# The up projection of the MLP as seven half-sized products with weight sums made in DRAM

## The chip, the cores and the metric

The kernel runs on one core of a Trainium2 chip. The metric is the device time of one execution in microseconds (us). All times are of this kernel with one set of inputs, and every array is float32.

## The reference

One decoder layer over 512 tokens of 1024 features. A combined input projection feeds three attention branches (differential, stick-breaking, dilated) and three gates; their merged output goes through a projection and a LayerNorm. Then comes the part that the change is about:

```python
x = layer_norm(DEEPNORM_ALPHA * x + m, ln1_g[i], ln1_b[i])
hid = jax.nn.relu(x @ w_up[i])                 # (512,1024) @ (1024,4096)
c = jnp.square(hid) @ w_down[i]                # (512,4096) @ (4096,1024)
ple = jax.nn.sigmoid(x @ w_ple_gate[i]) * (p[i] @ w_ple[i])
x = layer_norm(DEEPNORM_ALPHA * x + c + ple, ln2_g[i], ln2_b[i])
```

## The kernel before

**Products in three passes.** Each float32 factor is split into a high part in float32r and a low part (value minus high part, also in float32r). A product is hi x hi + hi x lo + lo x hi, three matmuls (`mm3`, L88 to L90) that accumulate in PSUM. A weight chunk of 128 x 1024 floats is loaded by SyncE into one of 7 `raw` buffers (`fill`, L162), cast to `wh` by ACT (L206) and subtracted to `wl` by DVE (L208). `wh` and `wl` have 7 buffers each; the split of a chunk may be written to the queues up to 7 chunks ahead of what the items have released (`pump`).

**Items.** The work of TensorE is a list of items, each with the chunks that it needs, a function `mm` that issues matmuls and a function `ev` that empties the bank. The loop at the end (L1352) goes through the list: it makes sure that the chunks are split, writes the previous item's `ev`, and then the item's `mm`. A scheduler then orders the instructions of each engine, so matmuls of neighbouring items can be interleaved. Items use two PSUM banks in turn (`mm_bank`); six more (`at_bank`) serve attention and long sums.

**MLP.** After the input projection, attention, the branches, the per-layer embedding (`ple_items`), the output projection (`wout_items`) and the gate (`pleg_items`) come `mlp_items`. The transposed input `x1T` (8 tiles of 128 features x 512 tokens, high and low part `x1Tl`) is made in `ln1_gen`. The up projection has 32 items `up(f)`, one for each 128 hidden columns: 8 feature tiles x 3 matmuls of 512 columns (tokens). Its `ev` makes relu and square on ACT.

The down projection is done in pairs of hidden tiles with a scheme of seven products for a 2 x 2 block product (in place of eight): tokens are cut in halves `HB` and `HC`, output columns in halves of 512. `left_first` and `left_rest` make the sums of the hidden activations on DVE and split them. `wsum` holds four sums of weight blocks for each of 7 groups of two pairs. They are made in DRAM by DMAs on POOL's queue: `sum_steps` copies a block and adds others to it in the transfer (L593, L595), 8 steps a group, one step per item from item 30 on, each tied to the latest `wl` subtraction. `down(b, p, r, c)` is product p for token tile r of its half: p = 1, 6, 7 stay in PSUM over all groups, the others are added to `acc` by DVE (L705) in each group. The eighth group is done in the plain way (`plain`), whose items also hold the second LayerNorm; the last item is cut in parts of 512, 256 and 256 columns.

**POOL's other work.** The loads of `pT` (L1000), of the LayerNorm constants (`ln_consts`) and of `xn`, and the power -0.5 of each LayerNorm (L440, L458) are on POOL's queue too, behind the sum steps that were written before them.

Of the kernel before, what the change touches and what calls it, by code (L numbers as in the profile page):

```python
# [56 lines left out]
def trunk(tc, a, out):  # L57
    nc = tc.nc
    es = ExitStack()
    with es:  # L60
# [7 lines left out]
        NSLOT = 42  # L68
# [74 lines left out]
        RING, RAW = 7, 7  # L143
# [332 lines left out]
        ln1_done = {}  # L476

# [22 lines left out]
        def ln1_gen(tt):  # L500
# [11 lines left out]
            for h in range(2):  # L512
# [7 lines left out]
            ln1_done[tt] = True  # L520
            yield
# [23 lines left out]
        def pleg_items():  # L545
            for half in range(2):
                cs = [chunk(a["wg"][half, c].rearrange("p k n -> p (k n)"), 1024) for c in range(4)]
                for tt in range(4):
# [9 lines left out]
                    def ev(ps, tt=tt, half=half):  # L558
# [6 lines left out]
                        if half and tt > 1:  # L565
                            nc.vector.tensor_sub(acc[tt - 2, 1], acc[tt - 2, 1], t)
# [9 lines left out]
        wsum = [[dram.tile([P, 1024], F32, name=f"wsum{b}_{i}") for i in range(4)] for b in range(7)]  # L576

        def sum_steps():
            def steps(b):
                w = [a["wd"][b, i].rearrange("p k n -> p (k n)") for i in range(4)]  # L580
                t = wsum[b]
                yield t[0], w[0], False
                yield t[2], w[1], False
                yield t[0], w[1], True
                yield t[2], w[3], True
                yield t[1], t[0], False
                yield t[1], w[3], True
                yield t[3], t[1], False
                yield t[3], w[2], True
# [10 lines left out]
            todo = deque(steps(b) for b in range(7))  # L600
            run = []
            while todo or run:
                while todo and len(run) < 3:
# [9 lines left out]
        hraw = {}  # L613
        later = deque()
        left = {}
        keep = {}
        p1s = {}
        v3 = {}
        HB = slice(0, 256)
        HC = slice(256, 512)  # L620

        def mlp_items():
            nb = 7

            def up(f, free=True):
                c = chunk(a["wu"][f].rearrange("p k m -> p (k m)"), 1024)

                def mm(ps):
                    for k in range(8):
                        s = slice(k * P, k * P + P)  # L630
                        mm3(ps, c["h"][:, s], c["l"][:, s], x1T[k], x1Tl[k], k == 0, k == 7)

                def ev(ps):
                    t = slot("hid")
                    nc.scalar.activation(t, ps, AF.Relu)
                    nc.scalar.activation(t, t, AF.Square)
                    left_rest()
                    if f >= 4 * nb:
                        left[f] = split(t)
                        return  # L640
                    hraw[f] = t
                    if f % 2:
                        left_first(f // 2)
                item([c] if free else [], mm, ev)
                return c

            def split(t, cols=slice(0, 512)):
                h = slot("hh", F32R)
                lo = slot("hl", F32R)
                nc.scalar.copy(h[:, cols], t[:, cols])  # L650
                nc.vector.tensor_sub(lo[:, cols], t[:, cols], h[:, cols].bitcast(F32))
                return h, lo

            def left_first(pr):
                e, o = hraw[2 * pr], hraw[2 * pr + 1]
                s12 = slot("s12")
                nc.vector.tensor_sub(s12[:, HB], e[:, HC], o[:, HC])
                nc.vector.tensor_sub(s12[:, HC], e[:, HB], s12[:, HB])
                w = slot("hh", F32R)
# [843 lines left out]
```

## Time and profile before

| what | value |
|---|---|
| median of 3 runs | 1081.71 us (1080.97 to 1082.08) |
| the profiled execution's time | 1082.02 us |
| its span, first to last instruction | 1080.1 us |
| granted TensorE clock | 0.998 |
| TensorE busy, share of the span | 99% |
| DVE, ACT, POOL busy | 61%, 44%, 6% |
| bytes read and written in HBM | 143.21 MB, 31.48 MB |

The span is shorter than the time by 1.9 us, which lie outside the first and last instruction. In a row of the timeline the first number is the start in us from the span's beginning, the second the duration; PE is TensorE's matmuls, PEld its weight loads. In a group's row the numbers behind the bar are the busy time in us and the mean duration of one in ns, then the idle time before it and what ended it. Matmuls are pipelined: the next starts before the last has ended, so their pace is read from their starts.

### The profile page before, as it was taken

The page shows a single profiled execution, that of the slowest core. Times are in us where ns is not written, and L with a number is a line of the kernel's source. Part 1 is how long each engine was busy: PE and PEld are TensorE (multiplying, and loading weights), DVE is VectorE, ACT ScalarE, POOL GpSimd, SP SyncE. Part 2 cuts the span into 40 slices and gives each one's busy share as a digit, 9 for nine tenths or more (in the row PEclk, how much of TensorE's full clock was granted, in tenths as well). Part 3 has the DMA queues.
Part 4 walks back from the last instruction along what each step waited for, and adds up shares of the span by engine and source line. Part 5 has one row for each costly group of instructions (what it writes and reads, how often), then busy time and mean ns, then how long its engine had stood idle before and what let it go on. Part 6 is the DMA issues. An engine that isn't in the chain of part 4 may idle for free.

```text
span 1080.1 us, 13246 instructions
## 1 busy us (share of the span) xinstructions
PE 1069.5 (99%) x4986; PEld 893.5 (83%) x4986; DVE 661.1 (61%) x1223; ACT 478.5 (44%) x795; POOL 70.0 (6%) x111
## 2 busy tenths in 40 slices
PE   9999999999999999999999999999999999999997
PEld 6888788999888888888888888888888888888886
DVE  6888667547254757655443464864575575575676
ACT  6665545425232545464233332233555454454441
POOL 0000200000111011111110020110000000000000
PEclk9999999999999999999999999999999999999999
DMA  8332313153675354567873262242244343444302
GB/s 311 129 117 90 118 40 98 51 183 98 144 208 154 119 127 166 141 162 198 244 193 111 102 231 81 89 166 98 98 158 135 137 156 136 138 146 142 122 1 78
DMA packets 43520, 146.18 MB, mean 135 GB/s; under 512 B 5593, under 2 KB 6505, under 8 KB 43457
## 3 DMA queue, kind: packets, MB, share of 16 engines
q1 hardware_dynamic: 32448, 107.93, 29.4%
q0 software_dynamic: 10432, 36.50, 13.5%
q8 instruction: 39, 0.64, 0.2%
q10 hardware_dynamic: 576, 0.92, 0.2%
q14 instruction: 25, 0.20, 0.1%
HBM read 143.21 MB, written 31.48 MB: 162 GB/s over the span
## 4 chain that ended last, share of the span: by engine, by line
PE 96%; DVE 2%; DMA 1%; ACT 0%; issue 0%; SPq 0%; DVEq 0%
PE mm L88 18%; PE mm L89 18%; PE mm L90 18%; PE mm L317 3%; PE mm L319 3%; PE mm L318 3%; PE mm L698 2%; PE mm L699 2%; PE mm L700 2%; PE at L698 2%; PE at L699 2%; PE at L700 2%; PE mm L556 1%; PE mm L490 1%; PE mm L488 1%; PE mm L554 1%
## 5 line engine op out<-in xcount | busy, mean ns | idle before, releaser
L206 ACT CAST wh<-raw 128x1024 fp32r<-128x1024 f32 (+1 forms) x201 | 207.8, 1035 | 347.1 <-PE mm L89 274.5
L208 DVE TENSOR_TENSOR wl<-raw,wh 128x1024 fp32r<-128x1024 f32 (+1 forms) x201 | 241.0, 1201 | 181.4 <-ACT wh L206 176.9
L88 PE MATMUL mm<-xhT,wh 128*128 128x512 f32 x496 | 196.3, 396 | 0.0
L89 PE MATMUL mm<-xlT,wh 128*128 128x512 f32 x496 | 194.0, 391 | 0.0
L90 PE MATMUL mm<-xhT,wl 128*128 128x512 f32 x496 | 194.0, 391 | 0.0
L90 PEld LDWEIGHTS mm<-xhT,wl 128*128 128x128 f32 x496 | 93.2, 188 | 19.5
L88 PEld LDWEIGHTS mm<-xhT,wh 128*128 128x128 f32 x496 | 93.3, 188 | 18.4 <-issue 0.2
L89 PEld LDWEIGHTS mm<-xlT,wh 128*128 128x128 f32 x496 | 93.2, 188 | 18.2 <-issue 0.2
L88 PE MATMUL mm<-x1hT,wh 128*128 128x512 f32 x256 | 99.6, 389 | 0.0
L89 PE MATMUL mm<-x1lT,wh 128*128 128x512 f32 x256 | 99.6, 389 | 0.0
L90 PE MATMUL mm<-x1hT,wl 128*128 128x512 f32 x256 | 99.6, 389 | 0.0
L317 PE MATMUL mm<-wh,xhT 128*128 128x512 f32 x160 | 64.6, 404 | 0.0
L319 PE MATMUL mm<-wh,xlT 128*128 128x512 f32 x160 | 63.1, 395 | 0.0
L318 PE MATMUL mm<-wl,xhT 128*128 128x512 f32 x160 | 62.9, 393 | 0.0
L90 PEld LDWEIGHTS mm<-x1hT,wl 128*128 128x128 f32 x256 | 48.1, 188 | 10.0
L88 PEld LDWEIGHTS mm<-x1hT,wh 128*128 128x128 f32 x256 | 48.1, 188 | 10.0
L89 PEld LDWEIGHTS mm<-x1lT,wh 128*128 128x128 f32 x256 | 48.1, 188 | 9.9
L319 PEld LDWEIGHTS mm<-wh,xlT 128*128 128x128 f32 x160 | 37.9, 237 | 3.9
L318 PEld LDWEIGHTS mm<-wl,xhT 128*128 128x128 f32 x160 | 38.1, 238 | 3.5
L317 PEld LDWEIGHTS mm<-wh,xhT 128*128 128x128 f32 x160 | 37.9, 237 | 3.5
L698 PE MATMUL mm<-wh,hh 128*128 128x512 f32 x100 | 38.9, 389 | 0.0
L699 PE MATMUL mm<-wl,hh 128*128 128x512 f32 x100 | 38.9, 389 | 0.0
(353 smaller groups left out, 1899.3 us busy)
## 6 DMA issues: line engine op xcount, KB each, us to landing
raw<-in_wt_dram SPq DMA_DIRECT2D x62, 512.0 KB, 3.6
wsum<-in_wd_dram POOLq DMA_DIRECT2D x42, 512.0 KB, 7.3
raw<-in_wu_dram SPq DMA_DIRECT2D x32, 512.0 KB, 3.3
raw<-wsum SPq DMA_DIRECT2D x28, 512.0 KB, 3.3
raw<-in_wd_dram SPq DMA_DIRECT2D x25, 512.0 KB, 3.3
raw<-in_wv_dram SPq DMA_DIRECT2D x20, 512.0 KB, 4.3
wsum<-wsum POOLq DMA_DIRECT2D x14, 512.0 KB, 4.8
raw<-in_wb_dram SPq DMA_DIRECT2D x8, 512.0 KB, 4.1
```

Of the source, the lines that this page charges most:

```text
L88: nc.tensor.matmul(ps, wh, xh, start=start, stop=False, skip_group_check=True)
L89: nc.tensor.matmul(ps, wh, xl, start=False, stop=False, skip_group_check=True)
L90: nc.tensor.matmul(ps, wl, xh, start=False, stop=stop, skip_group_check=True)
L206: i = nc.scalar.copy(h, raw)
L208: i = nc.vector.tensor_sub(lo, raw, h.bitcast(F32))
L317: nc.tensor.matmul(ps, x1, c["h"][:, s], start=k == 0, stop=False)
L318: nc.tensor.matmul(ps, x1, c["l"][:, s], start=False, stop=False)
L319: nc.tensor.matmul(ps, x2, c["h"][:, s], start=False, stop=k == 7)
L488: nc.tensor.matmul(ps, h[:, q], c["h"][:, s], start=k == 0, stop=False)
L698: nc.tensor.matmul(ps, h[:, q], c["h"][:, s], start=go, stop=False, skip_group_check=True)
L699: nc.tensor.matmul(ps, h[:, q], c["l"][:, s], start=False, stop=False, skip_group_check=True)
L700: nc.tensor.matmul(ps, lo[:, q], c["h"][:, s], start=False, stop=end, skip_group_check=True)
```

## The change

- The up projection is done with seven products too. Pairs m = 0 to 7 of 512 hidden columns; each is done in two items i = 2m, 2m + 1. Tokens are cut in halves of 256, features in halves of 512 (4 tiles), hidden columns in halves of 128 per item. Each product is 4 tiles x 3 matmuls of 256 columns.
- `ln1_gen` also copies the transposed x1 to `raws`; `x_forms` and `last_form` make from it the sums and differences of blocks (`forms`), split in high and low parts. One of them overwrites a quarter of `x1T`.
- `usum` holds four sums of up weights for each pair, made in DRAM like `dsum` (the former `wsum`): 8 steps each, for 8 pairs of up and 7 of down, four generators in turn, from item 26 on, 4 steps in 3 items.
- An up item has four parts: a (products 2 and 1), b (7 and 6), c (5), e (3 and 4). Products 2, 1, 6, 5, 3 share one bank `b["x"]`, and between two of them ACT or DVE reads what is there so far (L716, L722, L733, L744); 7 and 4 share another, `b["y"]`.
- `hid[m]` has four tiles (128 x 512), one for each block; their sums for the down products are made by `left_step`, one product at a time, after parts of the down projection (`preps`).
- The down projection goes in stages: the ups of pairs [0], [1, 2], [3, 4], [5, 6], [7] beside the downs of [], [0], [1, 2], [3, 4], [5, 6]. Within a stage products 1, 6, 5, 3 are chained in one bank and 7, 4 in another, with DVE adding or subtracting the running sum in `acc` after each product; 2 stands alone. Products 2 and 4 of pairs 5 and 6 are done in `plain`, where pair 7 is done in the plain way.
- `RAW` goes from 7 to 4, `NSLOT` from 42 to 48, and the up weights have another layout in DRAM.

The core of the diff:

```diff
-        NSLOT = 42
+        NSLOT = 48
...
-        RING, RAW = 7, 7
+        RING, RAW = 7, 4
...
+                for kp in range(2):
+                    if tt % 2 == 0:
+                        raws[h, tt // 2, kp] = slot("x1r")
+                    r3 = raws[h, tt // 2, kp].rearrange("p (k t) -> p k t", k=2)
+                    nc.scalar.copy(r3[:, :, tt % 2 * P:tt % 2 * P + P], t3[:, 2 * kp:2 * kp + 2, :])
                 nc.scalar.copy(o, t3)
...
+            def part_a():
+                c = chunk(wu[:, 0:2, :].rearrange("p a n -> p (a n)"), 1024)
+                def mm(ps):
+                    if 1 not in forms:
+                        last_form()
+                    prod(ps[:, HC], 2, c, 512, True, True)
+                    b["s"] = slot("up")
+                    nc.scalar.copy(b["s"][:, HB], ps[:, HC])
+                    prod(ps[:, HB], 1, c, 0, True, False)
+                def ev(ps):
+                    if j == 0:
+                        hid[m] = [slot("hid") for _ in range(4)]
+                    nc.vector.tensor_add(hid[m][0][:, js], ps[:, HB], b["s"][:, HB])
+                item([c], mm, ev, bank=bank("x", mm_bank))
+            def part_b():
+                c = chunk(usum[m][0][j].rearrange("p a n -> p (a n)"), 1024)
+                def mm(ps):
+                    prod(ps[:, HB], 7, c, 0, True, False)
+                    prod(b["x"][:, HB], 6, c, 512, False, False)
+                def ev(ps):
+                    nc.scalar.copy(b["s"][:, HC], b["x"][:, HB])
+                    nc.scalar.copy(b["s"][:, HB], ps[:, HB])
+                item([c], mm, ev, bank=bank("y", at_bank))
+            def part_c():
+                c = cs[4] = chunk(usum[m][1][j].rearrange("p a n -> p (a n)"), 1024)
+                def mm(ps):
+                    prod(ps[:, HB], 5, c, 0, False, False)
+                def ev(ps):
+                    nc.vector.tensor_add(hid[m][3][:, js], ps[:, HB], b["s"][:, HB])
+                item([], mm, ev, need=[c], bank=lambda: b["x"])
+            def part_e():
+                c = chunk(wu[:, 2, :], 512)
+                def mm(ps):
+                    prod(b["x"][:, HB], 3, cs[4], 512, False, True)
+                    prod(ps[:, HB], 4, c, 0, False, True)
...
-                for k in range(8):
-                    s = slice(k * P, k * P + P)
-                    mm3(ps, c["h"][:, s], c["l"][:, s], x1T[k], x1Tl[k], k == 0, k == 7)
...
+        CHAIN = {1: ("x", True, False, (0, 0), 1), 6: ("x", False, False, (2, 0), 1), 5: ("x", False, False, (2, 1), -1),
+                 3: ("x", False, True, (0, 1), -1), 7: ("y", True, False, (2, 1), -1), 4: ("y", False, True, (2, 0), 1),
+                 2: ("z", True, True, (0, 0), 1)}
...
+            ups = [[0], [1, 2], [3, 4], [5, 6], [7]]
+            downs = [[], [0], [1, 2], [3, 4], [5, 6], []]
...
-            if n >= 30:
+            for _ in range((2 if n % 3 == 0 else 1) if n >= 26 else 0):
                 next(sum_steps_, None)
```

More of the change, by code (lines that the diff above doesn't have):

```diff
@@ L476, in trunk @@
         ln1_done = {}
+        ln2_at = [None]
         def wout_items():
@@ L520, in ln1_gen @@
             ln1_done[tt] = True
+            if tt == 3:
+                pending.append(x_forms())
             yield
@@ L598, in issue @@
                     mybir.DependencyClass.Sync, mybir.DependencyReason.DATA), reason="spread over the main stream")
-            todo = deque(steps(b) for b in range(7))
+            todo = deque()
+            for m in range(ND):
+                todo.append(up_steps(m))
+                if m < ND - 1:
+                    todo.append(down_steps(m))
             run = []
             while todo or run:
-                while todo and len(run) < 3:
+                while todo and len(run) < 4:
                     run.append(todo.popleft())
@@ L1363, in trunk @@
                 prev[0]["ev"](prev[1])
+                todo, lead = prev[0].get("then", ((), 0))
+                preps.extend(todo)
+                for _ in range(lead):
+                    left_step(*preps.popleft())
             pump(freed, {1: 3, 3: 0, 4: 0}.get(n, 1 if n < 10 else 2))
```

463 lines of the change are left out of this document (246 added, 217 removed).

## The prediction

> **What bounds the kernel now.** I read the page first, then the windows of the MLP, then the groups by line, then the timeline of the last matmuls. The page:
>
> ```profile
> span 1080.1 us, 13246 instructions
> PE 1069.5 (99%) x4986; PEld 893.5 (83%) x4986; DVE 661.1 (61%) x1223; ACT 478.5 (44%) x795; POOL 70.0 (6%) x111
> PEclk9999999999999999999999999999999999999999
> PE 96%; DVE 2%; DMA 1%; ACT 0%; issue 0%; SPq 0%; DVEq 0%
> L88 PE MATMUL mm<-x1hT,wh 128*128 128x512 f32 x256 | 99.6, 389 | 0.0
> q0 software_dynamic: 10432, 36.50, 13.5%
> wsum<-in_wd_dram POOLq DMA_DIRECT2D x42, 512.0 KB, 7.3
> wsum<-wsum POOLq DMA_DIRECT2D x14, 512.0 KB, 4.8
> raw<-in_wu_dram SPq DMA_DIRECT2D x32, 512.0 KB, 3.3
> ```
>
> The chain is TensorE from end to end, at full clock. L88 on x1hT, with L89 and L90 of the same count, is the up projection: 768 matmuls of 512 columns. A busy PE can still be waiting, so I looked at how many matmuls a stretch of the MLP holds:
>
> ```profile
> 720.00:820.00 100.00, 100.00 (x443) 82.84 (x442) 57.14 (x78) 45.06 (x62) 0.00 (x0) 1.00 0.38 130
> 820.00:920.00 100.00, 100.00 (x443) 82.84 (x442) 63.22 (x88) 50.24 (x68) 0.00 (x0) 1.00 0.41 140
> ```
>
> 443 in 100 us is one per 0.226 us. The timeline of the tail gives the pace of a stream without a wait, first and last row of 18 matmuls of 512 columns, then of 24 of 256:
>
> ```profile
> 1065.39 0.39 PE L743 MATMUL at<-wh,hh 128*128 128x512 f32 x1
> ...
> 1069.24 0.39 PE L753 MATMUL at<-wh,hl 128*128 128x512 f32 x1
> 1069.47 0.28 PE L751 MATMUL at<-wh,hh 128*128 128x256 f32 x1
> ...
> 1072.22 0.28 PE L753 MATMUL at<-wh,hl 128*128 128x256 f32 x1
> ```
>
> 17 steps in 3.85 us: 0.2265 us for 512 columns. 23 steps in 2.75 us: 0.1196 us for 256. The reader should see two things. The MLP already runs at the pace of its instructions (0.226 against 0.2265), so it holds no wait that a change could remove. And half the columns cost 53% of the time, not 50%.
>
> **Part 1, fewer columns on TensorE.** The up projection becomes 8 pairs x 2 halves x 7 products x 4 k-tiles x 3 = 1344 matmuls of 256 columns in place of 768 of 512. The down projection keeps its number of matmuls; the built orders differ in nothing else of size on this engine. So 1344 x 0.1196 - 768 x 0.2265 = 160.7 - 173.9 = **-13.2 us**, and all of it is on the path, because nothing else sets the pace there. The pace of 256 columns includes one weight load each:
>
> ```profile
> 1070.67 0.19 PEld L753 LDWEIGHTS at<-wh,hl 128*128 128x128 f32 x1
> 1070.79 0.19 PEld L751 LDWEIGHTS at<-wh,hh 128*128 128x128 f32 x1
> L89 PEld LDWEIGHTS mm<-x1lT,wh 128*128 128x128 f32 x256 | 48.1, 188 | 9.9
> ```
>
> A load lasts 0.19 us but the next starts 0.12 us later, so loads overlap and keep the pace. The Trainium skill (TensorE: Matmul & The Clock Gate, Back-to-back issue gap) gives 262 cycles for 256 columns and 518 for 512, an estimated 0.109 and 0.216 us, by which this term would be -19.0 us; the rows are 5 to 10% slower, and the sum goes by the rows. The same page's table of goals asks for dimensions of at least 512, which speaks against the change; the trace prices that at 0.1196 x 2 - 0.2265 = 0.013 us for each pair of halves.
>
> **Part 2, hand-offs on one PSUM bank.** Before, each up item fills a bank alone and two banks alternate. Now five products of an up item use one bank in the order 2, 1, 6, 5, 3, and between two of them another engine must read the bank: ACT copies after 2 (L716) and after 6 (L733), DVE adds after 1 (L722) and after 5 (L744). That is 4 hand-offs for each of 16 items, 64 in all, none of which exists in the trace of before. Such a hand-off costs the end of the last matmul (0.28 - 0.12 = 0.16 us past the slot of the next one), a hop, the read, and a hop back.
>
> ```profile
> 1069.67 0.69 DVE xn L772
> L660 ACT CAST hh<-hid 128x256 fp32r<-128x256 f32 x14 | 5.4, 388 | 0.0
> L657 DVE TENSOR_TENSOR s<-hid,hid 128x256 f32<-128x256 f32 x14 | 5.9, 425 | 0.0
> 989.43 1.05 ACT L206 CAST wh<-raw 128x1024 fp32r<-128x1024 f32 x1 [1.15 <-PE mm L700]
> 990.38 0.62 ACT L650 CAST hh<-s 128x512 fp32r<-128x512 f32 x1
> ```
>
> The hop: the 512-column matmul of 1069.24 ends at 1069.63 and L772 starts at 1069.67, 0.04 us. With reads of 0.39 (ACT) or 0.42 us (DVE) a hand-off needs 0.63 to 0.66 us if the reader is free. In the built order of TensorE other products stand in these gaps. Counting them at 0.12 and 0.2265 us, the gap 6 to 5 has never less than 1.3 us. But 21 gaps have under 1 us: 11 of the 16 after product 2 (0.48 to 0.96 us), 6 after product 1 (0.71 to 0.96), 4 after product 5 (0.80). There the reader must be free at once. It often isn't: casts and subtractions of weights stand in the same two queues, and a cast holds ACT for 0.95 us (989.43 to 990.38). From below the term is 0, if the order always puts the read ahead of the cast; a gain is excluded, since the MLP has no wait to lose. From above it is 21 x 0.95 = 20 us, a whole cast before each. With the engines busy two thirds (ACT) to three quarters (DVE) of the time (by the built queues and the durations of part 3's rows and their like, some 203 and 243 us in the MLP's 316 us of matmuls), a read arriving at random would find about a third of a cast ahead, and the order isn't random; I take a quarter, 0.24 x 21 = **+5 us**, nearer to the end where the order works, because the present MLP with its own tight queues waits nowhere.
>
> **Part 3, more work on DVE and ACT.** The weights of an up pair become 7 chunks, in place of 4. DVE by the groups of before:
>
> ```profile
> L208 DVE TENSOR_TENSOR wl<-raw,wh 128x1024 fp32r<-128x1024 f32 x88 | 107.4, 1223 | 104.2 <-ACT wh L206 103.2
> L705 DVE TENSOR_TENSOR xn<-xn,mm 128x512 f32<-128x512 f32 x50 | 34.1, 681 | 7.0 <-PE mm L700 7.0
> L651 DVE TENSOR_TENSOR hl<-s,hh 128x512 fp32r<-128x512 f32 x28 | 19.2, 687 | 4.3 <-ACT hh L650 4.2
> 987.80 1.23 DVE L208 TENSOR_TENSOR wl<-raw,wh 128x1024 fp32r<-128x1024 f32 x1
> 988.94 0.69 DVE L651 TENSOR_TENSOR hl<-s,hh 128x512 fp32r<-128x512 f32 x1
> 989.54 0.42 DVE L674 TENSOR_TENSOR s<-hid 128x256 f32<-128x256 f32 x1
> 989.88 0.42 DVE L675 TENSOR_TENSOR s<-hid,s 128x256 f32<-128x256 f32 x1
> ```
>
> Back to back they start 1.14, 0.60 and 0.34 us apart. The worst stretch of the built order is the last pair's up beside the downs of pairs 5 and 6: 14 subtractions of 1024, 29 operations of 512 and 5 of 256 columns, 35 us of DVE against 42 us of matmuls. That is 84%: hidden, but without much cover; were DVE a fifth slower in its waits for ACT, it would cost some 3 us. I book 0. The forms of x1 for the seven products (16 copies on ACT, 14 operations of 512 columns on DVE, 10 us) lie beside wout and the gate, where DVE has room:
>
> ```profile
> 625.00:690.00 65.00, 65.00 (x292) 53.62 (x291) 40.01 (x55) 17.57 (x21) 9.12 (x15) 1.00 0.43 146
> ```
>
> Two copies now precede each cast into x1T; uncovered they would cost 8 x 0.78 = 6 us, with the other tiles' matmuls between 0, which I take.
>
> **Part 4, loads and sums.** Four raw buffers in place of seven: a buffer is held for 3.3 us of landing, 1.05 of cast and 1.22 of subtraction, so four of them pass a chunk each 1.4 us, while the matmuls use one each 2.7 to 2.9 us (20.1 us for 7 chunks of an up pair). Hidden, even with landings twice as long. The sums made in DRAM rise from 56 steps to 120, on POOL's queue. The 56 steps of 0.52 MB (42 from the weights, 14 from a sum) are 29.4 of q0's 36.5 MB and so 117 of its 146 us (13.5% of the span): 2.1 us of all DMA engines a step, 134 us for 64 more.
>
> ```profile
> 200.00:570.00 370.00, 369.67 (x1824) 316.62 (x1823) 206.36 (x521) 155.82 (x326) 44.65 (x64) 1.00 0.58 160
> 570.00:625.00 55.00, 55.00 (x244) 45.58 (x243) 21.60 (x26) 17.88 (x25) 0.00 (x0) 1.00 0.31 104
> pTraw<-in_pT_dram POOLq DMA_DIRECT2D x1, 512.0 KB, 3.9
> 625.08 0.59 POOL L1000 DMA_DIRECT2D pTraw<-in_pT_dram  x1 [58.94 <-PE mm L90]
> 641.16 0.39 PE L535 MATMUL mm<-wh,pThl 128*128 128x512 f32 x1
> 681.60 1.01 POOL L440 TENSOR_TENSOR lr<-lr,mhalf 128x1 f32<-128x1 f32 x1 [39.19 <-DVE lr L439]
> POOL wsum L595 <- DVE wl L208: 183.2, 13, 99.5
> ```
>
> From 200 to 650 us the DMA engines then go from 54% to about 84%. The steps are issued until the wout items, so they now stand ahead of pT, xn and the first LayerNorm's power (L440) on POOL. pT is asked for 16 us before its first matmul and needs 3.9 of landing, 1.05 of cast and 1.22 of subtraction, so some 9 us of delay are covered; POOL itself spends its time waiting for its ticks from DVE (the last row), so it can catch up. I book 0.
>
> **Sum.** The profiled execution took 1082.02 us, 1080.1 of span and 1.9 around it, 0.3 above the median of 1081.71. 1082.0 - 13.2 + 5.0 = 1073.8, so 1073.5 for the median. The tail after the last matmul is the same code.
>
> **Rivals.** *Hand-offs eat the gain (slower).* 13.2 / 64 = 0.21 us lost at each hand-off, or 0.63 at each of the 21 tight ones, is the point from which the change loses. At 0.3 us for each of the 64, that is -13.2 + 19.2: 1087.7. For it: DVE above four fifths busy in the last stretch, and reads behind casts in order. Against it: the matmuls of other products that the built order puts between. In the built order product 1 waits for the copy of product 2, though the two use different columns of the bank, so this hand-off counts like the other three. The Trainium skill (PSUM — Partial Sum Buffer, PSUM bank collisions raise a hardware error) asks for just that, to guard PSUM by bank and not by address; no run so far shows it. *Sums late.* POOL falls behind the main stream and pT, xn or L440 come 20 us late, 10 of them uncovered: about 1083.5. Against it: POOL's long waits for DVE, above. *Weight loads bind.* At the 0.188 us of a load a matmul, the up takes 252.7 us, 78.8 more: about 1160. The tail's loads, 0.12 us apart, speak against it. *Half the columns at half the time.* 0.1133 us each makes the term 152.2 - 173.9 = -21.7, without waits 1060. The rows of 256 columns speak against it. The Trainium skill's section named in part 1 has a pace close to this.
>
> **How the numbers follow.** A measurement of this kernel tells about 0.2% (2.2 us) from no change. The forecast with 0 to 10 us of waits, 1068 to 1079, has 0.70; hand-offs 0.17; late sums 0.07; weight loads 0.03; the half pace 0.03. Faster: nearly all of the first, the last, and a few hundredths of late sums, 0.73. Same 0.05. Slower 0.22. The range 1067 to 1087 leaves out the weight loads, the half pace and the upper half of the hand-offs; the forecast's own range is 1068 to 1079.
>
> **What would show it.** Right: matmuls of 256 columns 0.12 us apart, 160 to 162 us in their streams, some 5 us of gaps after products 2, 1 and 5, ended by ACT L716 or DVE L722 and L744; the PE part of the chain still above 93%. Wrong: gaps above 13 us in all in the MLP; PE idle before L535 or the transposes at L515 with POOL as releaser; steps of 256 columns near 0.19 us; or waits on wl (L208) in the last stretch.

## The result and the profile after

The changed kernel takes **1120.36 us** (median of 4 runs, 1118.55 to 1121.48), the kernel before on the same chip 1081.8 us. The ratio is 1.0356, with a 95% interval of 1.0338 to 1.0374: 38.6 us slower. The forecast was 1073.5 us, 8 us faster. The profiled execution took 1119.24 us, with a span of 1117.5 us.

The page of the changed kernel (the parts that answer to those shown of before; busy times, slices of 28 us, queue q0, chain, DMA issues):

```profile
span 1117.5 us, 14767 instructions
PE 1076.4 (96%) x5562; PEld 919.2 (82%) x5562; DVE 704.8 (63%) x1270; ACT 524.3 (47%) x898; POOL 116.4 (10%) x175
PEclk9999999999989998999999998989999999999999
DMA  7332315376665656765999999862555565557532
q0 software_dynamic: 23744, 70.06, 27.0%
PE 88%; DVE 5%; DMA 4%; ACT 1%; issue 1%; SPq 0%; POOL 0%; DVEq 0%; POOLq 0%; ACTq 0%
usum<-in_wu_dram POOLq DMA_DIRECT2D x48, 512.0 KB, 10.2
dsum<-in_wd_dram POOLq DMA_DIRECT2D x42, 512.0 KB, 9.8
```

TensorE is no longer the whole chain (88% in place of 96%), it is idle for 1117.5 - 1076.4 = 41.1 us, where it was idle for 10.6, and its clock is down in several slices. The last steps of the change, the MLP, hold none of this. Where the time is lost is seen from when TensorE starts its stages, in us of the two traces:

| stage, first or last matmul | before | after | later by |
|---|---|---|---|
| first on the da tables' logits (`da_k`) | 362.6 | 369.4 | 6.8 |
| first of the branches (`oTh`) | 473.8 | 489.6 | 15.8 |
| last with `da_v` | 493.5 | 515.5 | 22.0 |
| first of the embedding (`pThl`) | 641.2 | 668.9 | 27.7 |
| first of the gate | 698.4 | 741.4 | 43.0 |
| last of the gate, start of the MLP | 742.8 | 785.7 | 42.9 |
| last matmul | 1072.2 | 1108.3 | 36.1 |

The MLP itself went from 329.4 to 322.6 us. Everything else was lost ahead of it, in stages whose matmuls the diff does not touch. What TensorE waited for, by the view of waits (in all, times, longest, us):

```profile
PE at L1278 <- DVE on L1272: 7.6, 4, 2.9
PE at L516 <- DVE xn L444: 6.1, 1, 6.1
PE at L1340 <- DVE r L1333: 5.9, 1, 5.9
PE mm L489 <- DVE xn L495: 2.6, 1, 2.6
PE mm L543 <- ACT pThl L1104: 1.9, 1, 1.9
```

None of these five exists before, and none of them is a wait for a weight. L1278 and L1340 are in the attention, L543 is the embedding, L489 the output projection, L516 the transposes after the first LayerNorm. In the program each of them has an instruction of POOL behind it or near it: the table loads `sh<-rv`, the power of L1270, the loads of pT and xn, the power of L440. All of these are in the queue in which the sum steps stand.

### The profile page after: what moved, and what is told of

Its sections match the earlier page's. It is cut to its first block, busy times and chain, and to the rows that moved or that the text cites. A ratio compares the mean times of both kernels' runs of the same rounds, so it can differ in the third digit from the quotient of the medians.

```text
span 1117.5 us, 14767 instructions
## 1 busy us (share of the span) xinstructions
PE 1076.4 (96%) x5562; PEld 919.2 (82%) x5562; DVE 704.8 (63%) x1270; ACT 524.3 (47%) x898; POOL 116.4 (10%) x175
## 4 chain that ended last, share of the span: by engine, by line
PE 88%; DVE 5%; DMA 4%; ACT 1%; issue 1%; SPq 0%; POOL 0%; DVEq 0%; POOLq 0%; ACTq 0%
PE mm L88 15%; PE mm L89 15%; PE mm L90 14%; PE at L787 4%; PE at L788 4%; PE at L789 4%; PE mm L317 3%; PE mm L319 3%; PE mm L318 3%; DMA usum<-in_wu_dram 3%; PE at L90 1%; PE at L89 1%; PE at L88 1%; DMA xn<-in_xn_dram 1%; DVE wl L208 1%; PE mm L564 1%
## 5 line engine op out<-in xcount | busy, mean ns | idle before, releaser
L206 ACT CAST wh<-raw 128x1024 fp32r<-128x1024 f32 (+1 forms) x233 | 233.7, 1005 | 327.6 <-PE mm L89 242.7
L208 DVE TENSOR_TENSOR wl<-raw,wh 128x1024 fp32r<-128x1024 f32 (+1 forms) x233 | 270.5, 1167 | 159.0 <-ACT wh L206 156.0
L787 PE MATMUL at<-wh,hh 128*128 128x512 f32 x188 | 74.2, 395 | 0.8 <-ACT hh L652 0.8
L88 PE MATMUL mm<-x1hT,wh 128*128 128x256 f32 x256 | 74.0, 289 | 0.0
L788 PE MATMUL at<-wl,hh 128*128 128x512 f32 x188 | 73.8, 392 | 0.0
L789 PE MATMUL at<-wh,hl 128*128 128x512 f32 x188 | 73.2, 390 | 0.0
L90 PE MATMUL mm<-x1hT,wl 128*128 128x256 f32 x256 | 72.3, 283 | 0.0
L89 PE MATMUL mm<-x1lT,wh 128*128 128x256 f32 x256 | 72.3, 282 | 0.0
L619 POOL DMA_DIRECT2D usum<-in_wu_dram x32 | 33.8, 1056 | 111.9 <-DVE wl L208 55.5
L789 PEld LDWEIGHTS at<-wh,hl 128*128 128x128 f32 x188 | 35.4, 188 | 7.5 <-DVE hl L653 0.4
## 6 DMA issues: line engine op xcount, KB each, us to landing
usum<-in_wu_dram POOLq DMA_DIRECT2D x48, 512.0 KB, 10.2
```

The source lines that it names most:

```text
L88: nc.tensor.matmul(ps, wh, xh, start=start, stop=False, skip_group_check=True)
L89: nc.tensor.matmul(ps, wh, xl, start=False, stop=False, skip_group_check=True)
L90: nc.tensor.matmul(ps, wl, xh, start=False, stop=stop, skip_group_check=True)
L206: i = nc.scalar.copy(h, raw)
L208: i = nc.vector.tensor_sub(lo, raw, h.bitcast(F32))
L619: i = nc.gpsimd.dma_start(o, i, accum_op=OP.add, max_dma_last_dim=4096)
```

## The experiments

Two theories. **Q**, the queue: the sum steps stand in POOL's queue ahead of other work, each waiting for its tick (`wl`, L208) or for an older step, so that work comes late, and the orders of DVE and ACT are made around it. **D**, the traffic: 120 steps of all 16 DMA engines make loads late, whoever issues them. A third suspect was the smaller edit, 4 raw buffers. Later came **R**: the rows of 2 KB of the new up steps.

**e1, buffers in the kernel before.** `RAW` from 7 to 4 and `NSLOT` from 42 to 48, nothing else.

> The kernel before with the changed one's buffers alone: RAW 4 in place of 7, NSLOT 48 in place of 42. The changed kernel reaches its first per-layer-embedding matmul 27.7 us late (668.9 against 641.2). Theory B (buffers): the fewer raw buffers and the more slots make that delay; this kernel then takes 1100 to 1110 us, with TensorE waits over 0.5 us between 300 and 530 us. Theory S (sums): the 64 added sum steps make it; this kernel then stays within 3 us of 1082.

Measured 1081.75 us, ratio 1.0003 (0.9991 to 1.0014). **e2, buffers in the changed kernel**, 7 and 42:

> The changed kernel with the buffers of before: RAW 7, NSLOT 42. Theory B: the 27.7 us before the embedding go, some 1092 us. Theory S: they stay, 1117 to 1123 us.

1120.27 us. The buffers are not the cause, neither way.

**e3, no sums.**

```diff
-            next(sum_steps_, None)
+            pass
...
-    c = chunk(usum[m][0][j].rearrange("p a n -> p (a n)"), 1024)
+    c = chunk(wu[:, 0:2, :].rearrange("p a n -> p (a n)"), 1024)
```

(and the same for the other loads of `usum` and `dsum`)

> The changed kernel without any sum step in DRAM: the chunks that held sums load plain weight blocks of the same size, so all matmuls, loads and splits stay and POOL's 120 transfers go; what it computes is no longer the layer. Theory S: both losses ahead of the MLP (27.7 us before the embedding, 15.2 from there to the last gate matmul) go, 1075 to 1080 us. Theory B: only the 15.2 go, some 1104 us.

1074.06 us, ratio 0.9932 (0.9910 to 0.9955). All five waits are gone:

```profile
span 1072.3 us, 14593 instructions
PE 1061.9 (99%) x5562; PEld 908.9 (85%) x5562; DVE 704.5 (66%) x1270; ACT 523.6 (49%) x898; POOL 31.8 (3%) x55
DMA  7332313133222113122333272233555556557532
```

So the sums hold the whole loss, and the two pages split it: TensorE's idle time is 41.1 against 1072.3 - 1061.9 = 10.4 us, 30.7 more; its busy time 1076.4 against 1061.9, 14.5 more, with the same 5562 matmuls. 30.7 + 14.5 = 45.2 us is the difference of the spans. Nearly all of the 14.5 are matmuls at half clock, which follow the waits: TensorE is busy for 27.0 us in such stretches, half of which, 13.5 us, full clock would have saved (last section).

**e4, fewer steps at a time.** One step an item, in place of 4 in 3 items.

> The changed kernel with one sum step per item from item 26 on in place of four steps in three items, so the last steps fall into the MLP's first 15 items and the DMA engines have a quarter less of them before it. Theory S: the share of the DMA engines between 475 and 700 us falls from over 0.9 to about 0.75, the stretch from the embedding to the last gate matmul shrinks from 116.8 to under 108 us and the attention part gains too, 1095 to 1108 us. Theory B: the attention part stays 27 us late, 1108 to 1115 us.

1145.88 us, ratio 1.0596 (1.0562 to 1.0629): the other way, and outside of both expectations. Its stages are the same as in the changed kernel up to the embedding (369.5, 489.0, 515.0, 668.5 us), with a quarter fewer steps per item. So the loss there doesn't go with the rate of the traffic. The steps that are put off then stand in the MLP, which takes 349.6 us in place of 322.6: its largest wait is TensorE for the copy of L716, 11.1 us, and ACT's casts wait 17.5 us for loads of `in_wu`. Which of the late sums held these up wasn't followed further.

**e5, the attention's work out of the queue.** The table loads through SyncE; the power on VectorE, by a shift and three Newton steps, twelve instructions of 0.16 to 0.17 us.

```diff
-                nc.gpsimd.dma_start(t.rearrange("p (h m) -> p h m", m=m),
+                nc.sync.dma_start(t.rearrange("p (h m) -> p h m", m=m),
...
-                nc.gpsimd.tensor_tensor(ss, ss, mhalf.to_broadcast([P, 4]), OP.pow)
+                rsq(nc, small, ss)
```

> The changed kernel with all 120 sum steps as they are, but two kinds of POOL work taken out of the queue that the steps stand in: the table loads sh<-rv go out through SyncE, and the power of L1270 is computed on VectorE (eleven small instructions, a shift and three Newton steps). Theory Q (what POOL and VectorE do for the attention stands behind sum steps, and the engines' orders are made around that): the attention loses nothing, last product with da_v back from 515.5 to 493 to 498 us, total 1094 to 1102; the loss between the embedding products and the last gate product (15 us) stays. Theory D (the DMA engines and HBM are loaded by the sums, whatever the order of the queue): 1117 to 1125, last da_v product still near 515.

1092.12 us, ratio 1.0101 (1.0086 to 1.0116), a little under the expected 1094 to 1102; the last `da_v` product is at 492.9 us, as without sums (492.6). D doesn't explain that: the sum steps are the same ones. What is left is what was left alone:

```profile
PE at L516 <- DVE xn L444: 6.1, 1, 6.1
PE mm L489 <- DVE xn L495: 3.2, 1, 3.2
PE mm L543 <- ACT pThl L1104: 1.9, 1, 1.9
```

**e13 and e14, one of the two edits each**, tell how the attention's loss divides.

> The changed kernel, sum steps as they are, with only the table loads sh<-rv through SyncE; the power of L1270 stays on POOL. If the two kinds of POOL work lose their parts separately: first product with da_k at 362 (369.4 in the changed kernel), then the same loss as there up to the last da_v product, 507 to 510, total 1109 to 1115. If the tables alone hold the whole loss of the attention: 493 and 1092 to 1096.

> The changed kernel with only the power of L1270 on VectorE; table loads stay on POOL. Separate parts: first product with da_k still at 369 to 370, last da_v product 500 to 502, total 1098 to 1104. If the power alone holds the loss: 493 to 496 and 1092 to 1097.

e13: 1110.49 us, 9.9 less than the changed kernel, first `da_k` product at 361.9, last `da_v` product at 507.3. e14: 1100.72 us, 19.6 less, 370.3 and 501.2. The parts are separate and add up: 9.9 + 19.6 = 29.5, together 28.2. How such a part comes about is seen in the timelines around 410 us. DVE, then POOL, of the changed kernel:

```profile
415.12 0.17 DVE L1269 TENSOR_SCALAR ms<-ms 128x4 f32<-128x4 f32 x1
424.03 1.23 DVE L208 TENSOR_TENSOR wl<-raw,wh 128x1024 fp32r<-128x1024 f32 x1 [3.22 <-ACT wh L206]
429.46 1.23 DVE L208 TENSOR_TENSOR wl<-raw,wh 128x1024 fp32r<-128x1024 f32 x1 [4.20 <-ACT wh L206]
430.72 0.69 DVE L1272 TENSOR_TENSOR on<-at,ms 128x512 f32<-128x512 f32 x1
```

```profile
419.69 0.91 POOL L619 DMA_DIRECT2D usum<-in_wu_dram  x1 [5.97 <-DVE wl L208]
420.29 1.39 POOL L1270 TENSOR_TENSOR ms<-ms,mhalf 128x4 f32<-128x4 f32 x1
```

DVE hands `ms` over at 415.3. POOL takes it 5 us later, because a sum step ahead of it waits 6 us for its tick. But the power is done at 421.7, and L1272, which needs nothing else from there, starts at 430.7: two subtractions stand ahead of it in DVE's order, each waiting for a cast that waits for TensorE to free a weight buffer, while TensorE soon waits for L1272. From L1269 to L1272 DVE's order has three subtractions in the changed kernel and one in the run without sums, where L1269 starts at 407.45 and L1272 at 413.18. So the 5 us in the queue cost nothing here; the 9 us behind them are the order that the scheduler wrote for DVE. It is so for all four L1272 of the changed kernel: DVE never sits idle before one of them. The wait at L1340 is of the same kind: DVE starts the work behind it (L1302) at 316.7, right behind the last of three subtractions, and in e15 below at 302.9, behind one.

**e6, only the place of the steps.**

```diff
-            for _ in range((2 if n % 3 == 0 else 1) if n >= 26 else 0):
+            for _ in range((2 if n % 2 == 0 else 1) if n >= 18 else 0):
```

> The changed kernel with only the place of the sum steps changed: three in two items from item 18 on (1.5 an item instead of 1.33, and eight items sooner), so that the last one stands at item 98, where the load of pT is issued, ahead of the ln1 constants, xn and the power of L440. Theory Q: the attention still loses its 22 us (last da_v product 512 to 518), the stretch from the first embedding product to the last gate product falls from 116.8 to about 102, total 1098 to 1106. Theory D: the same traffic in less time, 1118 to 1130.

1108.75 us, ratio 1.0249 (1.0232 to 1.0266), a little above the expected 1098 to 1106. The attention loses its 22 us still (last `da_v` product at 516.0); from the first embedding to the last gate product it takes 105.7 us, where the changed kernel takes 116.8 and before 101.7. L516 and L489 are gone from the list of waits, L543 is not. What stands around the LayerNorm in the changed kernel, DVE first, then POOL:

```profile
715.93 0.15 DVE L439 TENSOR_SCALAR lr<-mv 128x1 f32<-128x1 f32 x1
...
728.21 3.49 DVE L208 TENSOR_TENSOR wl<-raw,wh 128x1024 fp32r<-128x1024 f32 x3
...
735.70 2.73 DVE L444 SCALAR_TENSOR_TENSOR xn<-xn,lr,ln_b 128x512 f32<-128x512 f32 x4
```

```profile
681.50 0.55 POOL L473 DMA_DIRECT2D xn<-in_xn_dram  x1 [3.25 <-DMA usum<-in_wu_dram]
...
725.26 0.56 POOL L621 DMA_DIRECT2D usum<-usum  x1 [5.43 <-DMA usum<-in_wu_dram]
727.13 0.91 POOL L619 DMA_DIRECT2D usum<-in_wu_dram  x1 [1.31 <-DMA usum<-usum]
728.39 0.83 POOL L619 DMA_DIRECT2D dsum<-in_wd_dram  x1 [0.35 <-DMA dsum<-dsum]
730.85 0.87 POOL L619 DMA_DIRECT2D usum<-in_wu_dram  x1 [1.64 <-DVE wl L208]
731.43 2.90 POOL L440 TENSOR_TENSOR lr<-lr,mhalf 128x1 f32<-128x1 f32 x3
```

The first token tile's variance is ready at 716.1 and its power starts at 731.4, with three powers done in a row: POOL is late by 15 us, behind steps that wait for older steps to land. Yet this isn't what TensorE waits for at L516. DVE's order has L444 behind the three subtractions from 728.2 and behind the fourth token tile, so that DVE comes to it at 735.7 without having waited for POOL, and e10 below has the same wait of 6.1 us with a prompt POOL. The queue does cost the wait at L489: the loads of xn are issued one by one from 681.5, 45 us later than before (636.33), where TensorE's stream itself is 28 late. Three times POOL waits between them for an older step to land, and DVE's first L495 sits idle for 10.4 us until xn is there, at 696.85.

**e7, e5 and e6 together.**

> Both edits: table loads through SyncE, the power of L1270 on VectorE, and three sum steps in two items from item 18 on. All 120 sum steps are done. Theory Q: every loss ahead of the MLP is gone, 1074 to 1080, under the kernel before. Theory D: 1112 to 1125, since all of the traffic is still there, in fewer microseconds.

1080.09 us, ratio 0.9985 (0.9976 to 0.9995), at the upper end of what was expected. All 120 steps are done, and 40.3 of the 46.3 us between the changed kernel and the run without sums are back. Two waits at the embedding are left, L543 and L545, 1.9 and 1.2 us. pT needed 13.4 us from issue to landing there, in a stretch with DMA slices at 9 tenths; whether that is the cause, e9 tests.

**e8, all steps late**, three an item from item 66.

> The changed kernel with three sum steps an item from item 66 on and none before; table loads and powers stay on POOL. No sum step stands ahead of the table loads of item 41. Theory Q: attention undisturbed up to the first dilated and da heads (first da_k product 362, not 369.4; last da_v product 493 to 500), the whole loss moves behind it, where three steps an item (some 6.3 us of all DMA engines in an item of 5.5 us) are more than the engines do: total 1100 to 1150. Theory D: the loss before 450 us goes too, since no sums run then, but nothing else tells it from Q here; what tells them apart is whether the waits after 500 us name POOL's instructions (Q) or weights that landed late (D).

1226.64 us, ratio 1.1336 (1.1309 to 1.1362), more than expected. Nothing is lost up to the last `da_v` product (362.2, 473.4, 493.1 us). Then one wait holds most:

```profile
PE mm L543 <- ACT pThl L1104: 108.3, 1, 108.3
PE mm L489 <- DVE xn L495: 37.4, 1, 37.4
```

The load of pT, ready to go at 625 us in the kernel before, is issued at 730.23: the queue ahead of it had to be issued first. No wait for a weight behind the start is in the list. The delay is what stands ahead in the queue, and it falls on POOL's own loads.

**e9, front loaded**: e7 with two steps an item from item 18 to 57 and one from 58 on, so that fewer are in flight where pT is loaded.

> As the kernel with both edits (table loads through SyncE, power of L1270 on VectorE), but two sum steps an item from item 18 to 57 and one an item from 58 on: the same 120 steps, the last again at item 98, fewer of them in the stretch before pT where the DMA slices stood at 9 tenths (485 to 647 us). If the 5.6 us that are left over the run without sums come from DMA work queued ahead of pT (13.4 us from issue to landing there) and of ln1 and xn: pT lands in under 6 us, the first embedding product at 640 to 641 instead of 642.2, the last gate product at 742 to 744, total 1073 to 1077. If they come from somewhere else, for example from sum steps being done at all: 1079 to 1083.

1079.72 us, ratio 0.9983 (0.9974 to 0.9992): no gain over e7, although pT landed in 3.8 us. A miss that tells something. ACT's order, in this run:

```profile
637.68 1.05 ACT L206 CAST wh<-raw 128x1024 fp32r<-128x1024 f32 x1 [3.14 <-PE mm L89]
640.40 1.04 ACT L206 CAST wh<-raw 128x1024 fp32r<-128x1024 f32 x1 [1.67 <-PE mm L89]
641.35 1.04 ACT L1104 CAST pThl<-pTraw 128x1024 fp32r<-128x1024 f32 x1
```

pT was in its buffer at 628, but its cast stands in the order behind four casts of weights (629.5 to 640.4), each of which waits for TensorE. Without sums it is at 628.12. The order is fixed when the program is built, presumably by what the scheduler expected of a load behind sum steps; a faster load doesn't change it. The changed kernel has the same order and the same two waits:

```profile
650.78 0.58 POOL L1103 DMA_DIRECT2D pTraw<-in_pT_dram  x1 [14.18 <-PE mm L90]
```

POOL issues pT there as soon as TensorE has freed the buffer, 18.1 us ahead of the first embedding product (16.1 before), and it lands in 3.9 us. ACT casts it at 667.79, behind four casts of weights.

**e10, front loaded, with pT, the constants and xn through SyncE.**

> The front loaded kernel, with the loads of pT, the layer norm constants and xn put on SyncE's queue as well. If the queue that POOL issues into is what delayed them: within 2 us of the front loaded kernel when that one has no wait left, 1072 to 1077. If a busy set of DMA engines is what counts, no matter who issues, the same time too; against both, SyncE's own weight loads now stand behind the wait for a free xn buffer, and a loss of 3 to 10 us would name that.

1082.55 us, ratio 1.0009 (1.0000 to 1.0018), above the expected 1072 to 1077. The waits for pT are gone (embedding at 640.7, without sums 640.3), but L516 waits 6.1 us for L444 again: three subtractions stand ahead of it in DVE's order, at 693.16. POOL, with nothing ahead of it, takes the first power 0.1 us after it is ready:

```profile
681.12 1.00 POOL L440 TENSOR_TENSOR lr<-lr,mhalf 128x1 f32<-128x1 f32 x1 [76.96 <-DVE lr L439]
```

TensorE waits for no weight there, so the loss isn't that of SyncE's own loads standing behind those of xn.

**e11, everything off POOL**, with the steps where the change put them (the edit also moves the powers of the second LayerNorm):

> The changed kernel with its sum steps left exactly where the change put them (1.33 an item from item 26 on, the last in the MLP), and all other work taken off POOL from the tables on: table loads, pT, layer norm constants and xn through SyncE, the powers of L1270 and of the first layer norm on VectorE. Theory Q in full: no wait is left that names POOL, and with the DMA engines still at 9 tenths from 475 to 670 us the time is 1074 to 1082. If the busy DMA engines cost time by themselves, whoever issues the loads: pT and xn land late all the same, 1085 to 1095 (1092.1 is what is left with tables and L1270 alone).

1143.82 us, ratio 1.0589 (1.0556 to 1.0622), outside of both expectations. The attention is whole (493.2), but in the profiled execution, the slowest of the four, the MLP takes 388 us: with the loads and the powers moved, the scheduler wrote another order for it, and TensorE waits there again and again, 15.2 us of it for casts of weights. This run says nothing on Q or D; it shows how far an order can move by edits that are not in the MLP.

**e12, only pT through SyncE**, otherwise e9. One line:

```diff
-            nc.gpsimd.dma_start(raw[:, 0:2, :], a["pT"])
+            nc.sync.dma_start(raw[:, 0:2, :], a["pT"])
```

> The front loaded kernel (all 120 sum steps, two an item from item 18 and one from item 58; table loads through SyncE, power of L1270 on VectorE) with one more edit: the one load of pT goes out through SyncE, while ln1 and xn stay on POOL. In the front loaded kernel pT landed 3.8 us after its issue at 624.3 us, yet ScalarE cast it only at 641.35, behind three weight casts that stand ahead of it in ScalarE's order. If that order is what is left of the loss: cast near 628, no wait ahead of the first embedding product (it was 2.0 and 1.4 us), total 1075 to 1077.5 against 1079.7. If not: 1079 to 1081, with the wait elsewhere.

**1074.67 us** (1074.58 to 1075.08), ratio 0.9935 (0.9923 to 0.9948), just under the expected 1075 to 1077.5: faster than both kernels, 0.6 us above the run without sums, with all 120 steps done. TensorE's busy time is 1061.9 us, to the tenth what it is without sums.

**What was still open.** The kernel before has one step an item in the same queue, beside the same tables and powers, and loses nothing; e4 has one step an item and loses 22 us in the attention. The rows differ: a step of the down weights moves 128 rows of 4 KB, a step of the up weights, as the layout has them, 256 rows of 2 KB. On the chip this makes no difference that shows (10.2 and 9.8 us to landing). **e16, the up steps alone**, 64 of them, one an item from item 30:

> The changed kernel with the 64 up steps alone, in 2 KB rows as there, one an item from item 30 on as the kernel before has its down steps (done by item 94); the down chunks are loaded as plain blocks, so the down projection is not the layer's. Half of the sum traffic, and no step beside the loads of pT and xn. If the 2 KB rows decide: the attention loses 20 to 23 us all the same (last da_v product 513 to 517), total 1095 to 1106. If the number of steps or the traffic decides: as the kernel before, which has 56 steps at the same place and loses nothing, 1073 to 1078.

1105.59 us, ratio 1.0226 (1.0210 to 1.0241). Half of the traffic, the rate of the kernel before, and the attention loses 20.7 us against the kernel before (last `da_v` product 514.2 against 493.5), by the same two waits as in the changed kernel, L1278 7.6 and L1340 5.9 us. **e15, 4 KB rows**, all else as in the changed kernel:

```diff
-        usum = [[dram.tile([2, P, 2, 512], F32, name=f"usum{m}_{i}") for i in range(2)] for m in range(ND)]
+        usum = [[dram.tile([P, 2, 2, 512], F32, name=f"usum{m}_{i}") for i in range(2)] for m in range(ND)]
...
-                w = [a["wu"][2 * m:2 * m + 2, :, i, :] for i in range(4)]
+                w = [a["wu"][m][:, i].rearrange("p j n -> p (j n)") for i in range(4)]
...
-            wu = a["wu"][i]
+            wu = a["wu"][m][:, :, j, :]
```

(and the layout of the up weights in DRAM to match; SyncE's loads of up chunks, which belong to the MLP, become 2 x 128 rows of 2 KB)

> The changed kernel with the up weights laid out so that the two items of a pair lie side by side: a sum step of the up weights moves 128 rows of 4 KB, as the down steps do, in place of 256 rows of 2 KB. The 120 steps, their bytes, their places (1.33 an item from item 26 on) and all other work on POOL are as in the changed kernel; SyncE's loads of up chunks become 2 x 128 rows of 2 KB. If the 2 KB rows are what the orders of the engines were made around (the scheduler taking such a step for longer than it is): the attention loses nothing (last da_v product 492 to 495 us) without any other edit, total 1074 to 1092, the width being what the real waits of xn and the power of L440 behind the steps keep. If it is the number of steps and their place in the queue: the attention loses its 22 us again, 1115 to 1122.

1089.43 us, ratio 1.0068 (1.0055 to 1.0080). The attention is whole (last `da_v` product 492.9), with 120 steps, tables and powers on POOL as in the changed kernel: R holds. POOL takes the power of L1270 at 407.95, and DVE's L1272 starts at 413.43.

What the rows change is the order that is written at build time, and the traces show it. Take DVE's instructions up to the last `da_v` product, 742 of them, in the order of their starts, and count how many must be moved to get the order of the run without sums: 35 in the changed kernel, in e4, e6 and e16, but 4 in e15 and e17, and none in e8, whose steps come later. From there to the last gate product it is 19 of 187 in the changed kernel and none in e15, e17 and e12. Why the scheduler orders so isn't seen; it looks as if it took a step of 2 KB rows for much longer than it is.

One large wait is left, of TensorE for L444, 9.8 us, and here the trace names POOL itself. DVE, then POOL:

```profile
682.40 0.15 DVE L439 TENSOR_SCALAR lr<-mv 128x1 f32<-128x1 f32 x1
...
694.96 1.41 DVE L444 SCALAR_TENSOR_TENSOR xn<-xn,lr,ln_b 128x512 f32<-128x512 f32 x2 [11.08 <-POOL lr L440]
```

```profile
686.24 0.52 POOL L621 DMA_DIRECT2D usum<-usum  x1 [3.02 <-DMA usum<-in_wu_dram]
688.77 0.84 POOL L619 DMA_DIRECT2D usum<-in_wu_dram  x1 [2.01 <-DMA usum<-usum]
691.22 0.83 POOL L619 DMA_DIRECT2D dsum<-in_wd_dram  x1 [1.61 <-DMA dsum<-dsum]
693.51 0.81 POOL L619 DMA_DIRECT2D usum<-in_wu_dram  x1 [1.46 <-DMA usum<-usum]
694.06 0.86 POOL L440 TENSOR_TENSOR lr<-lr,mhalf 128x1 f32<-128x1 f32 x1
```

The power waits 11.5 us behind steps that each wait for an older step to land. **e17, 4 KB rows and the early place of e6**, nothing taken off POOL:

> The wide rows of the run before, and the sum steps three in two items from item 18 on, so that the last stands at item 98, ahead of the loads of pT and xn and the power of L440; all other work stays on POOL. What is left in the run with wide rows alone is one wait, 9.8 us at L516 for L444, where the power of L440 and xn stand behind steps. If that is the rest of the loss: no wait of over 1 us in the list but those at the start, half clock at 7 to 9 us, total 1074 to 1077. If the steps cost something wherever they are: 1080 to 1085.

1075.54 us (1075.16 to 1075.94), ratio 0.9944 (0.9930 to 0.9957). No wait over 1.3 us is left. The window of 485 to 650 us (time, busy times of PE, PEld, DVE, ACT and POOL, clock, DMA share, GB/s):

```profile
485.00:650.00 165.00, 165.00 (x736) 136.30 (x735) 79.27 (x97) 58.06 (x79) 39.12 (x59) 1.00 0.98 267
```

The DMA engines are 98% busy over 165 us, more than in the changed kernel (0.90), and TensorE is busy for all of it. That decides against D: with all of the traffic the time is 1.5 us above the run without sums. Of the 46.3 us that the sums cost, the 2 KB rows and the orders made around them hold 30.9, and the place of the steps in the queue holds 13.9, which e15 still has and e17 hasn't.

## Why the prediction was wrong

**Part 1, the columns: right.** The forecast was -13.2 us, from steps of 0.1196 us. In the changed kernel 14 steps of 256 columns go from 785.94 to 787.61:

```profile
785.94 0.28 PE L88 MATMUL mm<-x1hT,wh 128*128 128x256 f32 x1
...
787.61 0.28 PE L90 MATMUL mm<-x1hT,wl 128*128 128x256 f32 x1
```

0.1193 us each. The MLP became 6.8 us shorter than its 329.4, where parts 1 and 2 together said 8.2. The rivals *weight loads bind* and *half the columns at half the time* are out. The Trainium skill's 262 cycles (TensorE: Matmul & The Clock Gate, Back-to-back issue gap), an estimated 0.109 us, differ, and the measurement decides.

**Part 2, the hand-offs: the size right, the places in part.** Forecast 5 us, at most 20. Steps more than 0.03 us longer than the median of their width hold 4.9 us over it in the MLP of the changed kernel (the longest 0.94, at L787), none before. 3.4 us of them lie at starts that waited for L716, L733 or L722 and in the step right behind such a start. But L733 ends seven of these waits, where the forecast saw a gap of 1.3 us or more and no cost, L744 none, and 1.2 us lie at L787 behind the cast of L652, for which there was no term. The forecast took a quarter of a cast at 21 places without a row for it, and that the sum agrees to 0.1 us is in part luck. The rival *hand-offs eat the gain* is out.

**Part 3, DVE and ACT: right.** From the first embedding to the first gate product it takes 57.2 us before and without sums, so the forms of x1 are hidden. In the stretch of the last pair's up, 1026.5 to 1068.5, DVE was busy for 36.2 of the 42 us, 86%, near the forecast of 84%, and TensorE for all 42.

**Part 4, buffers: right** (e1, e2). **Part 4, sums: the step that failed.** It booked 0, and the rival *sums late* had 10 us and a chance of 0.07; they cost 46.3 us (1120.36 against 1074.06). Where it went wrong:

- *All steps were taken as alike.* 64 more steps were priced by the bytes of the old ones. The new ones have rows half as long. On the chip both landed alike (10.2 and 9.8 us), but the order of the engines was made around it: with 4 KB rows alone the time falls by 30.9 us (e15), and with the early place as well by another 13.9 (e17). The part read the built order of TensorE in the MLP; DVE's and ACT's orders in the stages ahead of it were not compared with those before.
- *Whom it was looked for at.* The part named pT, xn and L440, where steps newly stand ahead. It didn't go through POOL's queue in the attention: the table loads and L1270, with the orders made around them, hold 28.2 us (e5).
- *How a delay was priced.* For pT the part weighed a delay of the load against a cover of 9 us. The load wasn't late; the cover was lost in ACT's order, behind casts of weights. Of the five waits of the changed kernel four are such orders, and one, 2.6 us at L489, is a load that the queue held up.
- *That the queue catches up.* "POOL can catch up" counts a queue as late by what it has to do. An instruction behind a chain of steps is late by their waits for each other: 11.5 us at L440 in e15, where the order no longer hides it and TensorE waits for 9.8 us, and over 100 us at pT in e8.
- *That a wait costs more than itself.* Some 13.5 us of the spans' 45.2 come from matmuls at half clock.

The signs listed as "wrong" did come: TensorE idle before L543 (L535 before) and at the transposes of L516. The releaser that the trace names there is ACT or DVE, not POOL, since what was late was their own order.

The rest of the sum is met, with the luck named in part 2: 1073.5 us predicted, 1074.06 without the sums, 1074.67 (e12) and 1075.54 (e17) with all of them.

## What to carry to other kernels

A background stream of DMAs on an engine's queue is priced by that queue and by the orders that are built around it, not by the busy share of the DMA engines. Where a scheduler writes the orders, compare the built order of every engine with the one before, also in stages that the diff doesn't touch, since an order keeps a loss even where the chip is early; that was the larger part here. Then list every instruction that shares the queue over its whole life, and give each the waits of the steps ahead of it. Keep the transfers of such a stream in the shape that the old ones had, and let it end before the first load on its queue that the main stream waits for.

## What was not expected of the hardware

**The clock after a wait.** After several of its waits TensorE ran at half clock for some microseconds. Windows of the changed kernel (the clock is the third number from the end):

```profile
320.60:324.70 4.10, 4.10 (x12) 3.38 (x13) 0.98 (x7) 2.16 (x9) 0.00 (x0) 0.50 0.98 247
431.40:437.00 5.60, 5.54 (x22) 5.15 (x23) 5.04 (x13) 3.15 (x8) 0.38 (x1) 0.50 1.07 230
697.60:703.00 5.40, 5.40 (x24) 4.48 (x25) 1.94 (x3) 0.00 (x0) 1.30 (x3) 1.00 0.88 277
```

The first follows a wait of 5.9 us, the second one of 2.9; the third a wait of 2.6, and it has full clock. From 7 us on to its last matmul the changed kernel has 34.1 us at half clock, in six stretches of 3.41 or 6.83 us, and the kernel before has none (behind the last matmul both have it, for 6.3 and 7.4 us). In these stretches TensorE is busy for 27.0 us, so that 31 us of waits cost some 13.5 us more. The Trainium skill (TensorE: Matmul & The Clock Gate, Part 1: The HAM clock gate) says that the clock is halved after an idle window of about 3.4 us and that the window runs freely. The lengths of the stretches agree, one or two such windows; the wait of 2.9 us that was enough is shorter than the window, and which of the shorter waits are hit can't be told from their length: a pair of 1.9 and 1.2 us at the embedding was followed by half clock in the changed kernel and by full clock in e9.

**Loads beside a full set of DMA engines.** In the slices at 8 and 9 tenths SyncE's loads did land late: 9.3 us for the output projection's weights and 11.0 for the gate's (median in the changed kernel), against 3.2 and 3.8 before. TensorE waited for none of them. Four raw buffers, passed on at one chunk in 2.7 us or more, cover an estimated 11 us (4 x 2.7).
